# Hymba step: two feed-forward rows started together on four weight tiles, and the next weights loaded in another order

## The chip, the cores and the metric

The kernel runs on one NeuronCore of a Trainium2 chip. A core has engines that work side by side, each in the order of its own instruction list: TensorE (PE, matrix products), VectorE (DVE), ScalarE (ACT), GpSimd (POOL) and SyncE (SP, which here only issues DMAs). The metric is the device time of one execution in microseconds, smaller is better; the time before is the median of three runs.

## The reference

One layer of a decoder, for 512 prompt tokens and 8 sequences of 4 new tokens (544 columns in all), width 1024, feed-forward width 2816, in float32:

```python
def swiglu(x, wg, wu, wd):
    return (jax.nn.silu(x @ wg) * (x @ wu)) @ wd

x = layer_norm(ALPHA * x + 0.5 * swiglu(x, ffn1_wg, ffn1_wu, ffn1_wd), ln1_g, ln1_b)
proj = x @ w_in                   # RWKV-7 heads and a short convolution
...                               # state update, group norm, gates
x = layer_norm(ALPHA * x + mix, ln2_g, ln2_b)
x = layer_norm(ALPHA * x + 0.5 * swiglu(x, ffn2_wg, ffn2_wu, ffn2_wd), ln3_g, ln3_b)
```

The change is in the first `swiglu`, and in the loading that the second shares with it.

## The kernel before, in words

**Three products for one.** Each float32 matrix is split into a high part (`hl[:, 0]`, written by ACT with rounding to the format `F32R`) and a low part (`hl[:, 1]`, the difference, written by DVE). `wsplit` does it for weights (L133, L134), `split` for inputs (L137, L138). A product is then three matmuls: high by high, high by low, low by high (`mm3`, L149 to L151).

**The feed-forward layers.** The class `Ffn` works on the 2816 hidden values in 22 rows of 128. Each row has a tile of gate weights (`"g"`) and one of up weights (`"u"`), 512 KB each. `up(m, h)` computes row m for half h of the columns (half 0 is columns 0 to 255, half 1 is 256 to 543): 24 matmuls with the gate tile, the silu on ACT (L324), 24 with the up tile, the multiplication on DVE (L328). Rows 0 to 3 are chunk 0 and are computed so, directly. Later chunks are computed in pairs of rows with fewer products, from sums and differences of weight blocks: `pairs` and `downs` go through `prod` (L464 to L466), and a table of events, sorted by due time, says when each combined weight is made. A counter `t` counts the products; each piece of weights is loaded (`load`, L407 and L409) as x and a, the block b is split off the x, a GpSimd DMA adds another block to the x in place (L437, L443), a and x are split, DVE adds a into the x (L430, L431), and the y so made is split too. Evacuations of PSUM in these parts are L525, L531, L534, L570 and L573 on ACT.

**Buffers in turns.** Raw weights come into five buffers of 512 KB that are used strictly in turns, in the order in which the program asks for them (`ring`); the split tiles use six others in the same way. A DMA whose buffer is still in use waits on SP, and what stands behind it on SP waits too. `feed(n)` asks for pieces as long as fewer than n are held, then makes those that are due. In layer 1 (`nf` = 2) the first half of rows 0 and 1 comes ahead of `main`; rows 2 and 3 are done in `main`, which asks for the weights of each row when it gets there. After row 2 `main` sets `t` to -5 and calls `feed(2)`, so that the first four pieces (two of down weights for each of two groups) are asked for ahead of row 3's tiles. In layer 2 (`nf` = 4) all rows' weights are asked for ahead of `main`.

**The order of work.** The code is a recording: a scheduler arranges each engine's instructions by its own estimate of times, and on each engine they then run in that order. The instruction orders below are the result of that.

## Time and profile before

| | |
|---|---|
| median of three runs | 1148.94 us |
| the runs | 1146.88, 1148.94, 1152.93 us |
| profiled execution | 1144.4 us, span 1142.3 us, mean granted clock 0.992 |
| PE busy | 1106.8 us (97%) |
| DVE busy | 857.2 us (75%) |
| ACT busy | 586.1 us (51%) |
| first matmul of the first half of row 0 | 4.72 us |
| first matmul of the second half of row 0 | 20.85 us |

Times within the profile count from the start of the span. A row of the timeline gives the start, the length, the engine (SPq is SP's queue), the line of the kernel, the operation with the tiles it writes and reads, and in brackets how long the engine had been idle and what ended that. `hl` and `hlb` are split weights, `raw` are weights as loaded, `xhl` is the split input, `tv` and `hhl` are split inputs of the later chunks, `cpb` and `sv` are scratch. A matmul's length in the row overlaps with the next, so the distance from start to start is what PE needs for one.

### The profile page before, as it was taken

The page shows a single profiled execution, that of the slowest core. Times are in us where ns is not written, and L with a number is a line of the kernel's source. Part 1 is how long each engine was busy: PE and PEld are TensorE (multiplying, and loading weights), DVE is VectorE, ACT ScalarE, POOL GpSimd, SP SyncE. Part 2 cuts the span into 40 slices and gives each one's busy share as a digit, 9 for nine tenths or more (in the row PEclk, how much of TensorE's full clock was granted, in tenths as well). Part 3 has the DMA queues.
Part 4 walks back from the last instruction along what each step waited for, and adds up shares of the span by engine and source line. Part 5 has one row for each costly group of instructions (what it writes and reads, how often), then busy time and mean ns, then how long its engine had stood idle before and what let it go on. Part 6 is the DMA issues. An engine that isn't in the chain of part 4 may idle for free.

```text
span 1142.3 us, 22932 instructions
## 1 busy us (share of the span) xinstructions
PE 1106.8 (97%) x9300; PEld 1049.3 (92%) x9300; DVE 857.2 (75%) x1602; ACT 586.1 (51%) x1066; POOL 174.2 (15%) x282
## 2 busy tenths in 40 slices
PE   8999999999999999999999999899999999999995
PEld 7999999999999999898788878899999999999995
DVE  7677988879776867745577368988979888787755
ACT  6545555564553476553245343657555555545523
POOL 0021131312100032221011100001222212121000
PEclk9999999999999999999999999999999999999998
DMA  8557594957742242262128423353675949577302
GB/s 281 119 112 168 131 219 116 200 149 166 163 145 78 92 132 66 53 121 78 48 66 223 118 76 96 130 184 63 130 180 124 228 97 217 148 161 167 105 1 79
DMA packets 97626, 149.32 MB, mean 131 GB/s; under 512 B 35056, under 2 KB 58992, under 8 KB 97520
## 3 DMA queue, kind: packets, MB, share of 16 engines
q1 hardware_dynamic: 70320, 111.67, 32.3%
q0 software_dynamic: 27200, 36.18, 20.2%
q8 instruction: 73, 1.20, 0.4%
q14 instruction: 33, 0.27, 0.1%
HBM read 129.17 MB, written 9.75 MB: 122 GB/s over the span
## 4 chain that ended last, share of the span: by engine, by line
PE 68%; DMA 10%; DVE 10%; issue 7%; ACT 5%; SPq 0%; ACTq 0%; POOL 0%; POOLq 0%; DVEq 0%
PE mm L149 7%; PE mm L464 7%; PE mm L151 7%; PE mm L465 6%; PE mm L466 6%; PE mm L150 6%; DMA raw<-in_gu 6%; PE sm L464 5%; PE sm L466 5%; PE sm L465 5%; DVE hl L134 2%; ACT hl L133 2%; PE sm L929 1%; DMA z<-in_xT 1%; PE sm L208 1%
## 5 line engine op out<-in xcount | busy, mean ns | idle before, releaser
L134 DVE TENSOR_TENSOR hl<-raw,hl 128x1024 fp32r<-128x1024 f32 (+3 forms) x228 | 269.5, 1189 | 67.0 <-ACT hl L133 64.8
L133 ACT ACTIVATE hl<-raw 128x1024 fp32r<-128x1024 f32 (+3 forms) x228 | 231.5, 1027 | 86.2 <-DVE raw L431 32.5
L149 PE MATMUL mm<-xhl,hl 128*128 128x256 f32 (+1 forms) x768 | 235.6, 307 | 8.4 <-ACT xhl L137 4.9
L151 PE MATMUL mm<-xhl,hl 128*128 128x256 f32 (+1 forms) x768 | 227.8, 298 | 1.4 <-DVE hl L134 1.4
L150 PE MATMUL mm<-xhl,hl 128*128 128x256 f32 (+1 forms) x768 | 226.4, 295 | 0.6 <-DVE xhl L231 0.3
L149 PEld LDWEIGHTS mm<-xhl,hl 128*128 128x128 f32 x768 | 147.4, 192 | 16.6 <-ACT xhl L137 5.2
L150 PEld LDWEIGHTS mm<-xhl,hl 128*128 128x128 f32 x768 | 147.5, 192 | 6.5 <-issue 1.6
L151 PEld LDWEIGHTS mm<-xhl,hl 128*128 128x128 f32 x768 | 147.0, 192 | 5.8 <-DVE hl L134 2.4
L464 PE MATMUL sm<-xhl,hl 128*128 128x272 f32 x432 | 124.7, 289 | 0.0
L466 PE MATMUL sm<-xhl,hl 128*128 128x272 f32 x432 | 124.6, 289 | 0.0
L465 PE MATMUL sm<-xhl,hl 128*128 128x272 f32 x432 | 124.6, 288 | 0.0
L464 PE MATMUL mm<-tv,hl 128*128 128x272 f32 x288 | 83.7, 291 | 3.5 <-ACT cpb L525 2.9
L466 PE MATMUL mm<-tv,hl 128*128 128x272 f32 x288 | 83.6, 290 | 0.0
L465 PE MATMUL mm<-tv,hl 128*128 128x272 f32 x288 | 82.5, 286 | 0.0
L466 PEld LDWEIGHTS sm<-xhl,hl 128*128 128x128 f32 x432 | 81.6, 189 | 0.0
L443 POOL DMA_DIRECT2D raw<-in_wd x32 | 39.3, 1494 | 277.2 <-DVE hlb L138 275.4
L465 PEld LDWEIGHTS sm<-xhl,hl 128*128 128x128 f32 x432 | 81.3, 188 | 0.0
L464 PEld LDWEIGHTS sm<-xhl,hl 128*128 128x128 f32 x432 | 81.3, 188 | 0.0
L437 POOL DMA_DIRECT2D raw<-in_gu x36 | 43.4, 1206 | 238.4 <-DVE hlb L138 131.7
L464 PEld LDWEIGHTS mm<-tv,hl 128*128 128x128 f32 x288 | 54.1, 188 | 5.0 <-ACT cpb L525 3.5
L464 PE MATMUL mm<-hhl,hl 128*128 128x272 f32 x192 | 57.0, 302 | 1.7 <-ACT sv L570 1.6
L464 PE MATMUL sm<-hhl,hl 128*128 128x272 f32 x192 | 55.9, 291 | 0.0
(367 smaller groups left out, 2818.9 us busy)
## 6 DMA issues: line engine op xcount, KB each, us to landing
raw<-in_gu SPq DMA_DIRECT2D x86, 512.0 KB, 5.0
raw<-in_gu POOLq DMA_DIRECT2D x36, 512.0 KB, 7.4
raw<-in_wd SPq DMA_DIRECT2D x32, 512.0 KB, 4.8
raw<-in_win SPq DMA_DIRECT2D x26, 512.0 KB, 3.6
raw<-in_wd POOLq DMA_DIRECT2D x32, 256.0 KB, 6.5
raw<-in_wd SPq DMA_DIRECT2D x16, 384.0 KB, 3.3
z<-cpb POOLq DMA_DIRECT2D x16, 272.0 KB, 8.7
z<-sv POOLq DMA_DIRECT2D x16, 272.0 KB, 5.7
```

The source lines that it names most:

```text
L133: ACT.activation(hl[:, 0, a:b], raw[:, a:b], AF.Copy)
L134: DVE.tensor_tensor(hl[:, 1, a:b], raw[:, a:b], hl[:, 0, a:b].bitcast(F32), op=OP.subtract)
L149: PE.matmul(out, wh, src[:, 0, k, c0:c1], start=(i == 0), stop=False)
L150: PE.matmul(out, wh, src[:, 1, k, c0:c1], start=False, stop=False)
L151: PE.matmul(out, wl, src[:, 0, k, c0:c1], start=False, stop=(i == n - 1))
L208: PE.matmul(v[:, :n], ones, qq[:, i, :], start=(j == 0 and i == 0), stop=(j == 3 and i == 1))
L437: POOL.dma_start(x.rearrange("p (s c) -> p s c", s=2), bass.AP(tensor=a11.tensor, offset=a11.offset, ap=[[2 * D, P], [P * 2 * D, 2], [1, 5 ...
L443: POOL.dma_start(four(x)[:, i], bass.AP(tensor=a11.tensor, offset=a11.offset, ap=[[DFF, P], [P * DFF, 2], [1, 256]]), accum_op=OP.add)
L464: PE.matmul(out, wh, src(0, i), start=(first and i == 0), stop=False, skip_group_check=True)
L465: PE.matmul(out, wh, src(1, i), start=False, stop=False, skip_group_check=True)
L466: PE.matmul(out, wl, src(0, i), start=False, stop=(i == n - 1), skip_group_check=True)
L929: PE.matmul(q[r0:r0 + m, o:o + nn], lhs, rhs, start=True, stop=True)
```

## The change

The first half of rows 0 and 1 is no longer done tile after tile. All four weight tiles come in pieces of two, two and four of the eight input blocks, interleaved with the input, and `first_rows` goes through the input blocks in pairs and takes the four tiles in turns for each pair, with four accumulators in PSUM. Ahead of it come an activation with one element (which loads ACT's silu table), a memset and four full-precision matmuls on zeros whose result is not used. In `main`, layer 1 asks for row 3's tiles after row 1, and both layers ask for up to five pieces ahead instead of two. The same products are computed, with the same sizes.

```diff
+        def first_rows(self, o):
+
+            for a, b in ((0, 2), (2, 4), (4, 6), (6, 8)):
+                for i in range(4):
+                    hl = self.w["gu"[i % 2], i // 2]
+                    for k in range(a, b):
+                        for j, (v, y) in enumerate(((0, 0), (0, 1), (1, 0))):
+                            PE.matmul(o[i][:, :256], block(hl, v, k), xhl[:, y, k, 0:256], start=(k == 0 and j == 0),
+                                      stop=(k == KD - 1 and j == 2), skip_group_check=True)
+            for m in range(2):
+                s = self.rows[0][:, m, 0:256]
+                ACT.activation(s, o[2 * m][:, :256], AF.Silu)
+                DVE.tensor_tensor(s, s, o[2 * m + 1][:, :256], op=OP.mult)
+            yield 0
+
...
                 yield from self.up(m, 1)
                 next(tv)
-                if i == 2 or i == 1 and self.nf == self.na:
+                if i == 1 and self.nf < self.na:
+                    for j, n in enumerate("gu"):
+                        self.w[n, 3] = wload(self.gu[3, :, j, :])
+                elif i in (1, 2):
                     self.t = (-12, -5)[i - 1]
-                    self.feed(2)
+                    self.feed()
...
     f1.open()
-    raw, hl = wtiles()
-    f1.w["g", 0] = hl
+    ACT.activation(warm, one, AF.Silu)
+    POOL.memset(cpb[:, 0:256], 0.0)
+    firsts = [sm() for _ in range(4)]
+    for _ in range(4):
+        PE.matmul(firsts[0][:, :256], cpb[:, 0:P], cpb[:, 0:256], start=True, stop=True)
+    ws = [wtiles() for _ in range(4)]
+
+    def first_w(i, a, b):
+        raw, hl = ws[i]
+        dma(raw[:, a * P:b * P], gu1[i // 2, :, i % 2, a * P:b * P])
+        wsplit(hl, raw, a * P, b * P)
+
+    def first_x(a, b, c0, c1):
+        dma(z[:, a:b, c0:c1], xT[:, a:b, c0:c1])
+        split(xhl[:, 0, a:b, c0:c1], xhl[:, 1, a:b, c0:c1], z[:, a:b, c0:c1])
+
+    for a, b in ((0, 2), (2, 4), (4, 8)):
+        first_w(0, a, b)
+        first_x(a, a + 2, 0, 256)
+        first_w(1, a, b)
+        if b - a > 2:
+            first_x(a + 2, b, 0, 256)
+        first_w(2, a, b)
+        first_w(3, a, b)
+    for i, key in enumerate((("g", 0), ("u", 0), ("g", 1), ("u", 1))):
+        f1.w[key] = ws[i][1]
     for k in range(0, KD, 2):
-        dma(raw[:, k * P:(k + 2) * P], gu1[0, :, 0, k * P:(k + 2) * P])
-        dma(z[:, k:k + 2, 0:256], xT[:, k:k + 2, 0:256])
-        wsplit(hl, raw, k * P, (k + 2) * P)
-        split(xhl[:, 0, k:k + 2, 0:256], xhl[:, 1, k:k + 2, 0:256], z[:, k:k + 2, 0:256])
-    f1.w["u", 0] = wload(gu1[0, :, 1, :], 1024, 2)
-    f1.w["g", 1] = wload(gu1[1, :, 0, :])
-    f1.w["u", 1] = wload(gu1[1, :, 1, :])
-    for k in range(0, KD, 2):
-        dma(z[:, k:k + 2, 256:T], xT[:, k:k + 2, 256:T])
-        split(xhl[:, 0, k:k + 2, 256:T], xhl[:, 1, k:k + 2, 256:T], z[:, k:k + 2, 256:T])
+        first_x(k, k + 2, 256, T)
+    for i, n in enumerate("gu"):
+        f1.w[n, 2] = wload(gu1[2, :, i, :])
     dma(vc, vec)
     dma(ones, cst[:, C_ONES:C_ONES + P])
-    drain(f1.first(), f1.main())
+    drain(f1.first_rows(firsts), f1.main())
```

**SP, the first weights and inputs.** SP's list at its beginning; the number behind a tile's name tells buffers' uses apart, in the order of the program. Before, a quarter of row 0's gate tile (`raw_91`) and a quarter of the input's first half (`z`) alternate, and the other three tiles come whole or in halves:

```order
L633 DMA raw_91<-in_gu1 128x256
L634 DMA z_77<-in_xT 128x2x256
L116 DMA raw_117<-in_gu1 128x512 x2
L116 DMA raw_125<-in_gu1 128x1024
L116 DMA raw_130<-in_gu1 128x1024
L641 DMA z_77<-in_xT 128x2x288 x4
```

Now (`raw_101`, `103`, `105` and `107` are the four tiles), the first and the last group:

```order
L657 DMA raw_101<-in_gu1 128x256
L661 DMA z_77<-in_xT 128x2x256
L657 DMA raw_103<-in_gu1 128x256
L657 DMA raw_105<-in_gu1 128x256
L657 DMA raw_107<-in_gu1 128x256
L657 DMA raw_101<-in_gu1 128x512
L657 DMA raw_103<-in_gu1 128x512
L657 DMA raw_105<-in_gu1 128x512
L657 DMA raw_107<-in_gu1 128x512
L661 DMA z_77<-in_xT 128x2x288 x4
```

Ahead of the input's second half (the last row of each) there were 12 DMAs, eight alternating quarters and four for the other three tiles; now there are 16, with the same bytes.

**SP, row 3's tiles and the pieces.** Before, from row 2's tiles on: `raw_535` and `raw_540` are row 3's, `511` to `533` the four down pieces, `681`, `683` and `685` the first pieces of chunk 1 (x and a of its first pair, x of its second), `769` and `771` the next two:

```order
L409 DMA raw_511<-in_wd1 128x2x512
L409 DMA raw_513<-in_wd1 128x2x512
L409 DMA raw_531<-in_wd1 128x2x512
L409 DMA raw_533<-in_wd1 128x2x512
L116 DMA raw_535<-in_gu1 128x1024
L407 DMA raw_681<-in_gu1 128x1024
L116 DMA raw_540<-in_gu1 128x1024
L407 DMA raw_769<-in_gu1 128x1024
L407 DMA raw_771<-in_gu1 128x1024
L407 DMA raw_683<-in_gu1 128x1024
L407 DMA raw_685<-in_gu1 128x1024
```

Now row 3's are `409` and `414`, the down pieces `539` to `545`, and chunk 1's `547`, `565`, `567`, `787`, `789`:

```order
L116 DMA raw_409<-in_gu1 128x1024
L116 DMA raw_414<-in_gu1 128x1024
L424 DMA raw_539<-in_wd1 128x2x512
L424 DMA raw_541<-in_wd1 128x2x512
L424 DMA raw_543<-in_wd1 128x2x512
L424 DMA raw_545<-in_wd1 128x2x512
L422 DMA raw_547<-in_gu1 128x1024
L422 DMA raw_565<-in_gu1 128x1024
L422 DMA raw_567<-in_gu1 128x1024
L422 DMA raw_787<-in_gu1 128x1024
L422 DMA raw_789<-in_gu1 128x1024
```

Row 3's tiles moved ahead of the down pieces, and chunk 1's pieces now come in the order in which they are used.

**ACT, rows 2 and 3.** `sv` is row 2's and 3's result, `hlb` the b block of a piece. Before, around row 2's silu:

```order
L133 ACTIVATE hl_536<-raw_535 128x1024
L137 ACTIVATE hhl_88<-hk_89 128x272
L137 ACTIVATE tv_256<-cpb_71 128x544
L133 ACTIVATE hl_526<-raw_511 128x1024
L324 ACTIVATE sv_90<-mm_391 128x256
L137 ACTIVATE hlb_712<-raw_681 128x512
```

Now:

```order
L137 ACTIVATE hlb_705<-raw_543 128x512
L137 ACTIVATE hlb_730<-raw_547 128x512
L324 ACTIVATE sv_90<-mm_419 128x256
L133 ACTIVATE hl_557<-raw_539 128x1024
L137 ACTIVATE hhl_88<-hk_89 128x272
L137 ACTIVATE tv_284<-cpb_71 128x544 x2
```

The split of the b block of chunk 1's first piece (`hlb_712`, now `hlb_730`) moved from behind row 2's first silu to ahead of it. From the end of chunk 0 on all engines have the same instructions in the same order as before, but for a few in the first pairs of chunk 1.

## The prediction

> **What bounds the kernel now.** The page comes first.

> ```profile
> span 1142.3 us, 22932 instructions
> PE 1106.8 (97%) x9300; PEld 1049.3 (92%) x9300; DVE 857.2 (75%) x1602; ACT 586.1 (51%) x1066; POOL 174.2 (15%) x282
> ```

> TensorE (PE) is busy 97% of the span, so the kernel ends when PE has issued its last matmul. The change can only take away time in which PE stands or issues slowly. The sum of busy and idle by stretch (columns: stretch, length, busy time and count of PE, PEld, DVE, ACT, POOL, granted clock, DMA share, GB/s) shows the beginning:

> ```profile
> 0.00:4.72 4.72, 0.00 (x1) 0.01 (x1) 0.45 (x2) 2.38 (x4) 0.40 (x8) 1.00 0.52 146
> 4.72:12.03 7.31, 6.84 (x25) 5.65 (x25) 5.04 (x9) 4.92 (x9) 0.00 (x0) 1.00 0.99 310
> 12.03:20.85 8.82, 8.79 (x73) 8.59 (x73) 6.87 (x11) 5.92 (x10) 0.00 (x0) 1.00 1.05 380
> 20.85:48.00 27.15, 27.15 (x215) 27.15 (x214) 20.95 (x38) 17.65 (x30) 5.01 (x4) 1.00 0.68 165
> ```

> Busy time misleads here: 24 matmuls fill 4.72 to 12.03, and 72 of the same size fill the 8.82 us behind it. Next to the pitch of starts, the timeline of PE shows where it stood (start, length, instruction, and in brackets the idle time and what ended it):

> ```profile
> 4.72 0.58 PE L149 MATMUL mm<-xhl,hl 128*128 128x256 f32 x1 [4.72 <-ACT xhl L137]
> 11.60 0.41 PE L150 MATMUL mm<-xhl,hl 128*128 128x256 f32 x1
> 11.82 0.38 PE L151 MATMUL mm<-xhl,hl 128*128 128x256 f32 x1
> 12.03 0.28 PE L149 MATMUL mm<-xhl,hl 128*128 128x256 f32 x1
> 12.15 0.28 PE L150 MATMUL mm<-xhl,hl 128*128 128x256 f32 x1
> 20.85 0.30 PE L149 MATMUL mm<-xhl,hl 128*128 128x288 f32 x1
> 48.31 0.28 PE L151 MATMUL mm<-xhl,hl 128*128 128x256 f32 x1
> 49.13 0.39 PE L149 MATMUL mm<-xhl,hl 128*128 128x256 f32 x1 [0.54 <-ACT hl L133]
> 49.36 0.28 PE L150 MATMUL mm<-xhl,hl 128*128 128x256 f32 x1
> 50.39 0.39 PE L151 MATMUL mm<-xhl,hl 128*128 128x256 f32 x1 [0.76 <-DVE hl L134]
> 76.36 0.29 PE L465 MATMUL mm<-xhl,hl 128*128 128x272 f32 x1
> 78.27 0.39 PE L464 MATMUL mm<-hhl,hl 128*128 128x272 f32 x1 [1.62 <-ACT sv L570]
> 85.52 0.28 PE L466 MATMUL sm<-xhl,hl 128*128 128x272 f32 x1
> 88.40 0.39 PE L464 MATMUL mm<-tv,hl 128*128 128x272 f32 x1 [2.59 <-ACT cpb L525]
> 834.99 0.29 PE L466 MATMUL sm<-xhl,hl 128*128 128x272 f32 x1
> 836.25 0.39 PE L464 MATMUL mm<-tv,hlb 128*128 128x272 f32 x1 [0.98 <-ACT cpb L534]
> ```

> The pitch is 0.22 us at 11.60 and 0.12 us from 12.03 (8.82 / 72 = 0.1225 with one small wait, 0.1185 without). So the first half of rows 0 and 1 takes 20.85 - 4.72 = 16.1 us where 96 x 0.1185 = 11.4 us would do. Behind it come three stands in the first feed-forward layer, each counted as start to start less a pitch, plus 0.1 us for the slow start after it: row 3 loses (0.82 - 0.12) + (1.03 - 0.12) + 0.2 = 1.8 us, the one at 78.27 1.9 us, the one at 88.40 2.85 us. The last two rows are the second layer, to which I come back.

> What the three stands wait for is in the rows of SP, ACT and POOL:

> ```profile
> 42.78 0.33 SPq L116 DMA_DIRECT2D raw<-in_gu  x1
> 48.02 1.06 ACT L133 ACTIVATE hl<-raw 128x1024 fp32r<-128x1024 f32 x1 [0.24 <-DMA raw<-in_gu]
> 77.31 0.63 ACT L137 ACTIVATE hlb<-raw 128x512 fp32r<-128x512 f32 x1 [2.72 <-DMA raw<-in_gu]
> 78.96 1.21 POOL L437 DMA_DIRECT2D raw<-in_gu  x1 [5.00 <-DVE hlb L138]
> 85.11 2.95 ACT L133 ACTIVATE hl<-raw 128x1024 fp32r<-128x1024 f32 x3 [3.62 <-DMA raw<-in_gu]
> ```

> Row 3's second tile is issued only at 42.78, because its buffer (of five, in turns) holds the first down piece until that has been split. Its split at 48.02 is what PE waits for. Since row 3's two tiles stand in the turns behind four pieces, the third piece of the next chunk (the x of pair 1) comes into a buffer that is free only past 70 us: it lands at 77.3, its accumulating DMA leaves at 78.96 and lands at 85.1, and ACT, which works in order, has the evacuations for which PE waits (L570, L525) behind these two.

> **The change, part by part.**

> *The start.* Deliveries and splits are priced by these rows (DMA: count, size, time from issue to landing; two stretches, in which the flow begins; splits: mean ns of one):

> ```profile
> z<-in_xT SPq DMA_DIRECT2D x4, 256.0 KB, 4.5
> raw<-in_gu SPq DMA_DIRECT2D x4, 128.0 KB, 3.5
> 1.00:2.00 1.00, 0.00 (x0) 0.00 (x0) 0.00 (x0) 1.00 (x1) 0.00 (x0) 1.00 0.08 15
> 2.00:3.00 1.00, 0.00 (x0) 0.00 (x0) 0.00 (x0) 0.03 (x1) 0.00 (x0) 1.00 0.77 207
> 9.39 0.63 ACT L137 ACTIVATE xhl<-z 128x512 fp32r<-128x512 f32 x1 [0.27 <-DMA z<-in_xT]
> L133 ACT ACTIVATE hl<-raw 128x512 fp32r<-128x512 f32 x2 | 1.3, 631 | 0.0
> L134 DVE TENSOR_TENSOR hl<-raw,hl 128x512 fp32r<-128x512 f32 x2 | 1.3, 692 | 0.0
> ```

> The same 96 matmuls now stand in four groups of 24, and what they need together is four tiles of 512 KB and 1 MB of input, 3072 KB in 16 DMAs where the first tile and the input had 8. Before, the first 1536 KB had landed by 9.39. The other 1536 KB at the 380 GB/s of the 12.03 row take 4.0 us more: the last quarter pair lands at 13.4. Then 0.63 (ACT), 0.69 (DVE), four matmuls on that half (0.5) and the whole last group (24 x 0.1185 = 2.85): PE ends the first half at 18.1, and with small waits on the second half of the input at 18.35. That half has its own chain: DVE has to make four lower parts, with a plan input and two multiplications between; I get its last at 20.5, and PE needs it 18 matmuls into the next row, at 20.7. So it is just covered; a DVE that is 1 us later costs 0.8. Saved: 20.85 - 18.35 = **2.5 us**. The ends: at best PE runs fast from 5.4 on (5.4 + 11.4 = 16.8, **4.1 us**), at worst PE is slow until 12.03 as before: 31 matmuls at 0.21 from 5.44, then 65 x 0.1185, end 19.75, **1.1 us**. I lean to the middle since by the deliveries the clock hardly matters: a slow first group ends at 10.5, before the third group's tiles are there.

> *The warm-up.* It has to be free:

> ```profile
> L208 PE MATMUL sm<-lnq,ones 128*128 128x256 f32 x16 | 3.7, 386 | 1.4 <-ACT lnq L204 1.4
> L883 POOL MEMSET De<- 128x256 f32 x2 | 0.6, 310 | 39.8 <-DVE z L223 39.8
> ```

> The 16 rows are 8 full-precision matmuls, 0.46 us each at the fast pitch. Four of them at half speed take 3.7 us; behind a 0.31 us memset that can begin at 0.9 they run from 1.3 to 5.0, in the 4.72 us in which PE has nothing. Without that cover they cost 0.3 us. The early activation loads a table that ACT otherwise loads at 11.35; PE did not wait for that one, so I count nothing. What the row of 12.03 says of the clock is that PE was slow for 7.3 us of work with small gaps. [...]

> *Row 3 early.* Both tiles are issued right behind row 2's and split at about 27 and 30.5 us; row 3 begins at about 43. The 1.8 us go: **1.8 us**. If only the first tile came in time, 0.9.

> *Pieces in clean turns.* The two stands of 1.9 and 2.85 us go, and the question is what is late next. The second layer has just this order (all its weights ahead of all pieces), so it serves as price. From the first evacuation of its first chunk to that of the second:

> ```profile
> 64.98 0.40 ACT L570 ACTIVATE cpb<-mm 128x272 f32<-128x272 f32 x1 [1.57 <-PE mm L466]
> 133.94 0.40 ACT L570 ACTIVATE cpb<-mm 128x272 f32<-128x272 f32 x1 [1.59 <-PE mm L466]
> 808.49 0.40 ACT L570 ACTIVATE cpb<-mm 128x272 f32<-128x272 f32 x1 [1.11 <-PE mm L466]
> 874.28 0.40 ACT L570 ACTIVATE cpb<-mm 128x272 f32<-128x272 f32 x1 [1.60 <-PE mm L466]
> ```

> Layer 1 takes 68.96 us, layer 2 65.79: **3.2 us** between them. Layer 2 still has the stand at 836.25 (1.25 us), which layer 1 now hides behind its own. I expect it to come up at the same place, so the term is 3.2 and not 4.75. Ends: 4.75 if no stand comes up, 2.3 if two do.

> *The second layer* loads five pieces ahead instead of two. The instructions of every engine stand there in the same order as before, and SP reaches the DMAs no earlier than their buffers are free: nothing, and no more than its 1.25 us either way.

> **The sum:** 2.5 + 1.8 + 3.2 = 7.5 us. From the profiled execution, 1144.4 us (span 1142.3), that is 1136.9. This execution lies 4.5 us under the median 1148.94 of the three runs (1146.88 to 1152.93); from the median the forecast is **1141.4 us**. With the ends: 1.1 + 1.8 + 2.3 = 5.2 to 4.1 + 1.8 + 4.75 = 10.65, or 1143.7 to 1138.3.

> **The rivals.**

> *All stands go* and the start is at its best: 10.65 us, 1138.3. For it: the later chunks of layer 1 run without a stand. Against it: layer 2's stand in the same order.

> *PE stays slow to 12 us.* 1.1 + 1.8 + 3.2 = 6.1, 1142.8. For it: before, 7.3 us of work did not suffice. Against it: PE now works without a gap from 1.3.

> *The start is starved.* 16 smaller DMAs run at the rate of the first 1536 KB (from about 2.2, in the second of the two stretches, to 9.39: 213 GB/s) all the way: the last lands at 2.2 + 3072 / 213 = 16.6, PE ends at 21.3, 0.45 us after 20.85. Sum 4.55, 1144.4. For it: those rows, and four more DMAs ahead of the second input half. Against it: 380 GB/s as soon as rows of 2 KB and more come. [...]

> *Slower:* a piece ahead of its time stops ACT. The x of pair 0 is now split (hlb) ahead of row 2's first silu, and PE needs that silu for the third matmul group after it, at about 39.9. Its DMA leaves when DVE has split row 3's second tile, about 30.7, and by this row lands at 37:

> ```profile
> raw<-in_gu SPq DMA_DIRECT2D x5, 512.0 KB, 6.3
> ```

> So 2 us are spare, and from there each us costs PE one. It eats the gain from 9.5 us of lateness on; at 12 us (its buffer free only after layer 1's first y split, as row 3's tile had it) the time is 2.5 us above the median, 1151.4. For it: DVE is nearly full from 14 to 31 us. Against it: that buffer's last user in the new order is row 3's tile, not a piece.

> **How the numbers follow.** Likeliest 0.50; all go 0.15; slow clock 0.20; starved 0.10; slower 0.05. About 0.5% (5.7 us, below 1143.2) is what a measurement of this kernel tells from no change. The runs before spread over 6 us, so a median of three moves by some 2 us: faster then has 0.78 in the likeliest case, 0.95 when all goes, 0.55 with the slow clock, 0.4 when starved, in sum 0.68; I write 0.66, same 0.30, slower 0.04. The range takes the ends (1138.3 and 1144.4) and that 2 us on each side: 1136.5 to 1147.0.

> **What would show it.** Right: the first 128x288 matmul at about 18.3 us; no wait of row 3 on hl; from there to the first L570 of the next chunk no waits but one of about 1 us at the evacuation that is L534 now; the rest shifted as a whole by 7 to 8 us. Wrong: the first 128x288 matmul past 20; a wait of PE near 40 us behind a split of a piece; or a stand beyond 100 us that was not there. If the stands go and the end does not move, the later stages are not bound by PE as the 97% suggest.

## The result and the profile after

The changed kernel takes 1140.53 us in the median (1134.12 to 1150.78, 20 executions), the kernel before 1147.89 us (1143.24 to 1154.22, 20 executions on the same chip). The ratio is 0.9934 with a 95% interval of 0.9914 to 0.9955; of 1147.9 us the change saves 7.6, between 5.2 and 9.9. The forecast was 1141.4 us.

The page of the changed kernel begins so. Its profiled execution took 1138.5 us, 5.9 us less than the one before, and its span is 5.5 us shorter:

```profile
span 1136.8 us, 22970 instructions
PE 1107.5 (97%) x9308; PEld 1049.5 (92%) x9308; DVE 857.2 (75%) x1606; ACT 585.4 (51%) x1070; POOL 175.1 (15%) x283
```

The timeline of PE shows the start, the one stand that is left ahead of the second chunk's end, and the same place in the second layer:

```profile
1.25 3.78 PE L652 MATMUL sm<-cpb 128*128 128x256 f32 x8 [1.25 <-POOL cpb L649]
4.90 7.57 PE L360 MATMUL sm<-xhl,hl 128*128 128x256 f32 x49
12.80 5.83 PE L360 MATMUL sm<-xhl,hl 128*128 128x256 f32 x47 [0.34 <-DVE xhl L138]
18.47 0.30 PE L149 MATMUL mm<-xhl,hl 128*128 128x288 f32 x1
87.18 0.29 PE L481 MATMUL sm<-xhl,hl 128*128 128x272 f32 x1
90.28 0.39 PE L479 MATMUL mm<-tv,hlb 128*128 128x272 f32 x1 [2.81 <-ACT cpb L549]
828.63 0.29 PE L481 MATMUL sm<-xhl,hl 128*128 128x272 f32 x1
830.00 0.39 PE L479 MATMUL mm<-tv,hlb 128*128 128x272 f32 x1 [1.08 <-ACT cpb L549]
```

The first 128x288 matmul starts at 18.47 us (20.85 before). Row 3 no longer waits, and neither does PE at the two places in the second chunk where it stood for 1.9 and 2.9 us. But at the evacuation that is L549 now it stands for 3.10 us from start to start, where 1.25 us were forecast. SP and ACT show why (the SP row is the wait and issue of six DMAs in a row):

```profile
44.24 34.80 SPq L422 DMA_DIRECT2D raw<-in_gu  x6
86.83 0.63 ACT L137 ACTIVATE hlb<-raw 128x512 fp32r<-128x512 f32 x1 [4.95 <-DMA raw<-in_gu]
88.89 1.06 ACT L133 ACTIVATE hl<-raw 128x1024 fp32r<-128x1024 f32 x1 [1.42 <-DVE raw L446]
89.85 0.38 ACT L549 ACTIVATE cpb<-mm 128x272 f32<-128x272 f32 x1
```

The last of the six DMAs is issued at 79.04 (44.24 + 34.80) and lands at 86.83. ACT works in order and has the b split of this piece, the chunk's fourth, ahead of L549. Behind that split comes one that waits for DVE, and only then the evacuation for which PE waits.

What stands behind the stand is the surprise. The sum by stretch, for 3.9 us behind the stand in the changed kernel and then for 3.6 us behind the 2.9 us stand of the kernel before:

```profile
90.28:94.17 3.89, 3.89 (x18) 3.89 (x19) 3.89 (x5) 2.96 (x5) 0.00 (x0) 0.56 0.95 212
```

```profile
88.40:92.00 3.60, 3.60 (x28) 3.60 (x29) 3.56 (x6) 0.40 (x1) 1.21 (x1) 1.00 1.03 227
```

The granted clock is 0.56, and 18 matmuls start in the time of 31 at the full pitch of 0.126 us. Before, it stayed at 1.00. The stand costs 3.0 us, and the clock behind it 1.5 us more.

From here on one number serves as measure: the start of the first evacuation of the second chunk's end, which is the row of ACT that the prediction quoted at 133.94 us for before. With the change it is

```profile
129.84 0.40 ACT L585 ACTIVATE cpb<-mm 128x272 f32<-128x272 f32 x1 [1.59 <-PE mm L481]
```

so 4.1 us of the gain are made by then, in these two executions. Behind it no code differs that acts (the limit of five pieces in place of two gives the same instruction lists on all engines, row for row).

### The profile page after: what moved, and what is told of

It reads as the page before. It is cut to its first block, busy times and chain, and to the rows that moved or that the text cites. A ratio compares the mean times of both kernels' runs of the same rounds, so it can differ in the third digit from the quotient of the medians.

```text
span 1136.8 us, 22970 instructions
## 1 busy us (share of the span) xinstructions
PE 1107.5 (97%) x9308; PEld 1049.5 (92%) x9308; DVE 857.2 (75%) x1606; ACT 585.4 (51%) x1070; POOL 175.1 (15%) x283
## 4 chain that ended last, share of the span: by engine, by line
PE 72%; DVE 10%; DMA 8%; ACT 5%; issue 4%; SPq 0%; ACTq 0%; POOL 0%; POOLq 0%; DVEq 0%
PE mm L149 7%; PE mm L151 7%; PE mm L150 7%; PE mm L479 7%; PE mm L480 7%; PE mm L481 7%; DMA raw<-in_gu 6%; PE sm L479 5%; PE sm L480 5%; PE sm L481 5%; DVE hl L134 2%; ACT hl L133 2%; PE sm L964 1%; PE sm L208 1%; PE sm L149 1%
## 5 line engine op out<-in xcount | busy, mean ns | idle before, releaser
L134 DVE TENSOR_TENSOR hl<-raw,hl 128x1024 fp32r<-128x1024 f32 (+3 forms) x232 | 269.7, 1171 | 63.8 <-ACT hl L133 63.0
L133 ACT ACTIVATE hl<-raw 128x1024 fp32r<-128x1024 f32 (+3 forms) x232 | 232.0, 1012 | 81.6 <-DVE raw L446 33.3
L149 PE MATMUL mm<-xhl,hl 128*128 128x288 f32 (+1 forms) x736 | 224.2, 305 | 2.9 <-DVE z L1318 1.9
L151 PE MATMUL mm<-xhl,hl 128*128 128x288 f32 (+1 forms) x736 | 216.5, 295 | 0.6 <-DVE hl L134 0.6
L150 PE MATMUL mm<-xhl,hl 128*128 128x288 f32 (+1 forms) x736 | 214.8, 292 | 0.3 <-DVE xhl L231 0.3
L149 PEld LDWEIGHTS mm<-xhl,hl 128*128 128x128 f32 x736 | 139.1, 189 | 10.4 <-DVE z L1318 2.6
L150 PEld LDWEIGHTS mm<-xhl,hl 128*128 128x128 f32 x736 | 139.5, 190 | 5.2 <-issue 1.6
L151 PEld LDWEIGHTS mm<-xhl,hl 128*128 128x128 f32 x736 | 138.8, 189 | 4.6 <-issue 1.6
L479 PE MATMUL mm<-hhl,hl 128*128 128x272 f32 x192 | 57.0, 302 | 0.2
L480 PE MATMUL mm<-hhl,hl 128*128 128x272 f32 x192 | 55.7, 290 | 0.0
## 6 DMA issues: line engine op xcount, KB each, us to landing
raw<-in_gu SPq DMA_DIRECT2D x84, 512.0 KB, 5.0
raw<-in_gu POOLq DMA_DIRECT2D x36, 512.0 KB, 7.9
raw<-in_wd SPq DMA_DIRECT2D x32, 512.0 KB, 4.5
raw<-in_win SPq DMA_DIRECT2D x26, 512.0 KB, 3.6
raw<-in_wd POOLq DMA_DIRECT2D x32, 256.0 KB, 6.3
```

The source lines that it names most:

```text
L133: ACT.activation(hl[:, 0, a:b], raw[:, a:b], AF.Copy)
L134: DVE.tensor_tensor(hl[:, 1, a:b], raw[:, a:b], hl[:, 0, a:b].bitcast(F32), op=OP.subtract)
L149: PE.matmul(out, wh, src[:, 0, k, c0:c1], start=(i == 0), stop=False)
L150: PE.matmul(out, wh, src[:, 1, k, c0:c1], start=False, stop=False)
L151: PE.matmul(out, wl, src[:, 0, k, c0:c1], start=False, stop=(i == n - 1))
L479: PE.matmul(out, wh, src(0, i), start=(first and i == 0), stop=False, skip_group_check=True)
```

## The experiments

**Each half alone.** The first kernel has the new start and the old loading, the second the old start and the new loading:

```diff
 # start_only: the changed kernel with
-                if i == 1 and self.nf < self.na:
-                    for j, n in enumerate("gu"):
-                        self.w[n, 3] = wload(self.gu[3, :, j, :])
-                elif i in (1, 2):
+                if i == 2 or i == 1 and self.nf == self.na:
...
 # plan_only: the kernel before with the same lines the other way round
```

> The changed start alone; row 3's weights and the pieces as in the kernel before. Theory A (the gain is a sum of three separate parts, 2.4 us of it from the start): first 128x288 matmul at 18.5 us, and the stands of row 3 (1.8 us), of L570 (1.9) and of L525 (2.9) are all still there; the span is 2.4 us under that of before. Theory B (the parts depend on each other: rows that begin earlier reach row 3 earlier, while its second tile's buffer comes free at the same time): row 3's stand grows by what the start gained, to about 4 us, and the start alone gains under 0.7 us.

> The start as before; row 3's tiles ahead of the pieces, five pieces ahead. Theory A: first 128x288 matmul at 20.85 us as before, row 3 without a stand, then only the stand of 3.1 us at L534 (the line of the kernel before for L549); gain 1.8 + 4.75 - 3.1 = 3.5 us. Theory B (the stand at L549 is so long because everything now comes 2.4 us sooner): with the old start that stand is only about 1 us, as in layer 2, and this kernel alone gains 5 to 5.5 us, nearly all of the change.

The start alone: 1145.57 us, ratio 0.999 (0.9961 to 1.002). The loading alone: 1139.65 us, ratio 0.9913 (0.988 to 0.9947). By these times nearly all of the gain comes from the loading and next to none from the start. But the 2.4 us that the start was to save lie within the interval of the start alone, so the times do not decide between its theories. The trace speaks against theory B: row 3's stand, which was to grow to about 4 us, takes 1.92 us (1.61 before). The start itself does what it should, the first 128x288 matmul is at 18.66 us. PE of the kernel with the start alone then stands five times:

```profile
47.24 0.38 PE L149 MATMUL mm<-xhl,hl 128*128 128x256 f32 x1 [0.84 <-ACT hl L133]
48.50 0.38 PE L151 MATMUL mm<-xhl,hl 128*128 128x256 f32 x1 [0.76 <-DVE hl L134]
76.57 0.40 PE L479 MATMUL mm<-hhl,hl 128*128 128x272 f32 x1 [1.83 <-ACT sv L585]
86.69 0.40 PE L479 MATMUL mm<-tv,hl 128*128 128x272 f32 x1 [1.05 <-ACT cpb L540]
95.34 0.39 PE L479 MATMUL mm<-tv,hlb 128*128 128x272 f32 x1 [0.84 <-ACT cpb L549]
76.57:81.00 4.43, 4.43 (x23) 4.43 (x24) 3.17 (x6) 2.44 (x5) 1.21 (x1) 0.61 0.44 54
```

The stands are other ones than before but of the same sum, 6.15 us against 6.16 (each start to start, less a pitch of 0.12). What takes 1.6 us of the start's 2.2 back in this execution is the last row: behind the stand of 1.83 us the clock is halved. The kernel with the loading alone has one stand, of 1.39 us where its two theories had 3.1 and about 1, and no halved clock behind it:

```profile
91.40 0.39 PE L464 MATMUL mm<-tv,hlb 128*128 128x272 f32 x1 [1.22 <-ACT cpb L534]
91.40:94.81 3.41, 3.41 (x27) 3.41 (x28) 3.41 (x5) 2.84 (x5) 0.00 (x0) 1.00 0.88 216
87.96 0.63 ACT L137 ACTIVATE hlb<-raw 128x512 fp32r<-128x512 f32 x1 [3.37 <-DMA raw<-in_gu]
```

The clock also hides the start in the times. The record has the span and the mean granted clock of each of these executions. Their product is the span less the time that a halved clock cost, if PE was busy meanwhile, so it is an estimate of the time at full clock. In the mean it is 1133.9 us for the 15 executions of the kernel before, 1131.8 with the start alone and 1131.3 with the loading alone: 2.2 and 2.7 us less (standard errors 0.7 and 0.6). For the loading alone that is less than the 4.5 us that its trace has by the second chunk's end (129.42). Its five executions had lost less to the clock, 6.1 us in the mean against 12.0 before. By this the start is worth about what it was forecast to be.

**Without the warm-up.** The four matmuls on zeros are left out:

```diff
-    for _ in range(4):
-        PE.matmul(firsts[0][:, :256], cpb[:, 0:P], cpb[:, 0:256], start=True, stop=True)
```

> The change without the four matmuls on zeros. Theory A (the start is bound by deliveries: 256 KB each 0.69 us from 10.7 on): PE is at the slow pitch until 8 to 12 us, the first group ends at about 10 instead of 8.2, but the first 128x288 matmul is at 18.5 to 19.0, as good as unchanged. Theory B (the clock sets the start's end): slow until 12 us as in the kernel before, end at 19.7 or later, 1.2 us lost.

Measured: 1139.89 us, ratio 0.9912 (0.9881 to 0.9943), not to be told from the change. Two stretches of the start, without the warm-up and then with it, show what it does:

```profile
6.00:8.00 2.00, 2.00 (x12) 2.00 (x10) 1.16 (x3) 0.88 (x3) 0.00 (x0) 1.00 0.99 342
8.00:10.00 2.00, 2.00 (x12) 2.00 (x12) 1.46 (x4) 1.42 (x4) 0.00 (x0) 1.00 0.99 283
10.00:12.00 2.00, 2.00 (x20) 2.00 (x19) 1.29 (x3) 1.29 (x3) 0.00 (x0) 1.00 0.99 322
```

```profile
6.00:8.00 2.00, 2.00 (x20) 2.00 (x19) 1.00 (x3) 0.86 (x3) 0.00 (x0) 1.00 1.03 326
8.00:10.00 2.00, 1.88 (x13) 1.36 (x12) 1.45 (x4) 1.44 (x4) 0.00 (x0) 1.00 0.87 265
```

With it PE is at 20 matmuls in 2 us from 6 us on, but then starves at 8 to 10 us. Without it PE is slow until about 10 us and has work all the time. The first 128x288 matmul comes at 18.95 in place of 18.47: the warm-up is worth 0.5 us, since the deliveries bound the start.

**The stand at L549.** What ACT waits for there is a split that PE needs only later. This kernel has it three products later, in the table of lead times:

```diff
-LEAD_B = {0: 25, 1: 23}
+LEAD_B = {0: 25, 1: 23, 3: 15}
```

> The change with the b block of the fourth row pair member (u = 3) made 15 instead of 18 products ahead, in every chunk of both layers; on ACT the split then stands behind the evacuation L549 instead of ahead of it. Theory A (the stand of 3.1 us in layer 1 and of 1.4 us in layer 2 is ACT waiting in order for a piece that PE does not need yet): both stands go or fall under 0.3 us and the span is 4 us under that of the change. Theory B (the piece itself is late): PE stands later instead, at the product with that b block or with the y made after it, and the span stays within 1 us.

Measured: 1138.55 us, ratio 0.9893 (0.9828 to 0.9958). ACT now evacuates first, and the stand is gone in both layers:

```profile
84.94 0.38 ACT L549 ACTIVATE cpb<-mm 128x272 f32<-128x272 f32 x1
87.42 0.63 ACT L137 ACTIVATE hlb<-raw 128x512 fp32r<-128x512 f32 x1 [0.66 <-DMA raw<-in_gu]
125.58 0.40 ACT L585 ACTIVATE cpb<-mm 128x272 f32<-128x272 f32 x1 [1.59 <-PE mm L481]
```

The piece still lands at 87.4. The span of this execution, 1142.1 us, does not show the gain, since the clock is halved from 518.8 to 546.1 us, in code that is the same. So the stand came from the order on ACT together with a late piece, and the order alone removes it. The second chunk's end comes 4.3 us earlier than with the change, 8.4 us earlier than before.

**Why the piece is late.** Two additions into z run on the DMA engines just then. This kernel cuts them from 272 to 16 columns, in this group alone, and so leaves out part of layer 1's sum:

```diff
-                    POOL.dma_start(z[:, ds[q]:ds[q] + 2, TB:], cp[q], accum_op=OP.add)
+                    w = 16 if self.ph == "1" and (ci, g) == (0, 1) else TB
+                    POOL.dma_start(z[:, ds[q]:ds[q] + 2, TB:TB + w], cp[q][:, :, 0:w], accum_op=OP.add)
```

> The changed kernel, with two additions of layer 1 thinned: the two DMAs of L596 that add the second group of chunk 0 into z at about 80.5 us carry 16 columns in place of 272, so that part of layer 1's sum is left out. Order and waits stay as they are. Theory D (the DMA engines are shared): the x whose split stops ACT at 86.83 lands late because its 512 KB compete with those 544 KB; without them it lands 1.5 to 2 us earlier, at about 85, the stand at L549 shrinks from 2.8 to 1.3 us or less and the clock stays full behind it; first L585 of the second chunk at about 126.8. Theory E (the issue sets it): it lands at 86.8 and the stand stays 2.8 us; first L585 at 129.8.

Measured: 1143.34 us, ratio 0.995 (0.9912 to 0.9987). Theory D fell. The rows of ACT and PE:

```profile
86.23 0.63 ACT L137 ACTIVATE hlb<-raw 128x512 fp32r<-128x512 f32 x1 [4.26 <-DMA raw<-in_gu]
89.68 0.39 PE L479 MATMUL mm<-tv,hlb 128*128 128x272 f32 x1 [2.12 <-ACT cpb L549]
89.68:93.00 3.32, 3.32 (x26) 3.32 (x27) 3.32 (x5) 2.85 (x5) 0.00 (x0) 1.00 0.90 219
```

The piece, issued at 79.49, lands at 86.23. The changed kernel itself, profiled once more beside it, had it issued at 79.50, landed at 86.37 and a stand of 2.10 us of idle time. So those bytes are not the cause; the two additions still ran, so this does not say that they cost nothing. Over five traces the stand follows the time from issue to landing: 7.8 us and 3.10 us from start to start, 7.9 and 3.14 without the warm-up, 6.9 and 2.39, 6.7 and 2.41 here, 5.8 and 1.51 with the old start. What sets that time between 5.8 and 7.9 us is still open.

**The changed kernel and the later split, with more executions, and the later split with the old start:**

> The changed kernel itself, for comparison on the same chip. Theory C: 4.1 us from the traces and 2.6 us for the clock that the profiled execution before escaped, 6.7 us in all, ratio 0.994; its stand of 2.8 us halves the clock for 3.41 us in nearly every execution. Theory T: 4.1 us, ratio 0.9964. In its trace the stand at L549 of 2.8 us again, and behind it 14 or 15 matmuls at a pitch of 0.23 us.

> The changed kernel with the b split of each chunk's fourth piece asked for three products later (lead 15 in place of 18), once more and with more executions. In the traces so far the first L570 or L585 of layer 1's second chunk starts at 133.94 us before, 129.84 with the change, 125.58 with this. Theory C (the clock): a stand of PE also halves the clock for 3.41 us, worth 1.71 us, when about 1.45 us of it fall into one 3.41 us window of a raster that runs by itself. The two stands of 1.62 and 2.59 us in the kernel before would then do this in about 62% and 91% of its executions, (3.41 - 1.62 + 0.34)/3.41 and (3.41 - 2.59 + 2.28)/3.41, though the profiled one escaped both: 2.6 us that its trace does not show. Gain over before: 8.4 + 2.6 + 1.35 for layer 2's stand = 12.3 us, ratio 0.989. Theory T (the traces alone): 8.4 + 1.35 = 9.7 us, ratio 0.9915. No stand at the evacuation that is L549 in either layer, under both.

> The kernel before with the change in the loading of rows 2 and 3 and the later b split, and with the old start. Theory A: the start's 2.4 us count in full as soon as PE waits for no delivery behind it: the first 128x288 matmul at about 21.2 us (18.82 with the new start), the first L570 of the second chunk at 127.9 (125.58), the whole 2.4 us longer than with the new start. Theory B: the deliveries of the second chunk set the pace whatever PE does, and the start is lost there in any case: first L570 of the second chunk at 125.6 to 126.1, the same time as with the new start.

Measured in this order: 1144.73 us, ratio 0.9958 (0.9922 to 0.9994); 1135.73 us, 0.9874 (0.9835 to 0.9913); 1134.42 us, 0.9859 (0.9824 to 0.9894). By the traces the start counts in full once no stand is left: the second chunk's end is at 125.65 us with the new start and at 127.69 with the old one. The times do not show these 2.0 us, so the pair was taken again:

> The changed kernel with the later b split a third time, beside the one with the old start: does the start show in the times where no stand is behind it? Theory A: 2.0 us by the traces (first L585 of the second chunk at 125.6 against 127.7), so 2 us faster than the one with the old start. Theory B: no difference or the other sign, as in the first pair (1135.73 against 1134.42).

> The old start with the new loading and the later b split, again. First 128x288 matmul at 20.9 to 21.2, first L570 of the second chunk 106.8 us behind it, no stand between. Theory A: 2 us slower than with the new start. Theory B: the same or faster.

This time the new start gave 1128.88 us, ratio 0.9832 (0.979 to 0.9873), the old one 1134.42 us, 0.9876 (0.9831 to 0.9921). The traces repeat to 0.1 us (125.58 and 127.67). The first pair has the new start 1.3 us slower, the second 5.5 us faster: executions of one kernel spread over 5 to 17 us, and 2 us do not show in pairs of six. With the clock taken out as above they do: span times granted clock is 1122.6 us in the mean with the new start and 1124.7 with the old one in the first pair, 1121.5 and 1123.8 in the second. That is 2.1 and 2.3 us (standard errors 0.9 and 0.7), as the traces have it.

**Is it the idle time that halves the clock?** This kernel gives PE 16 matmuls to do during the stand, ahead of the product that waits for L549. Their result is not used:

```diff
+                if self.ph == "1" and ci == 1 and u == 0:
+                    fill = sm()[:, :TB]
+                    for _ in range(16):
+                        PE.matmul(fill, xhl[:, 0, 0, 0:P], xhl[:, 0, 0, 0:TB], start=True, stop=True, skip_group_check=True)
                 yield from prod(b1, u, "b", 0, tb(2), False)
```

> The changed kernel with 16 matmuls more, whose result is not used, ahead of the product that waits for the evacuation L549 in layer 1's second chunk. They take 16 x 0.126 = 2.0 us and stand where PE waits 2.1 to 2.85 us anyway; all other lists are the same. In eight of the traces so far the start of the second chunk's end (the first L570 or L585 of the chunk) is the start of the first 128x288 matmul, plus the stands, plus 106.8 to 106.9 us where the clock stayed full, or 108.35 to 108.55 where it was halved behind a stand. Theory C (it is PE's idleness within one 3.41 us window that halves the clock): the wait ends when it did, but is under 0.9 us of idle, so the pitch behind it is 0.126 from the start, and that rest is 106.8 to 107.0. Theory F (the slow matmuls behind the stand come from something else that the stand goes with: DMA traffic, operands, the evacuation): the pitch is 0.23 for some 14 matmuls again, rest 108.4.

Measured: 1138.48 us, ratio 0.9916 (0.9881 to 0.995). The rows of PE and the stretch behind them:

```profile
87.31 0.29 PE L481 MATMUL sm<-xhl,hl 128*128 128x272 f32 x1
87.44 2.16 PE L515 MATMUL sm<-xhl 128*128 128x272 f32 x16
90.17 0.39 PE L479 MATMUL mm<-tv,hlb 128*128 128x272 f32 x1 [0.57 <-ACT cpb L553]
90.17:93.58 3.41, 3.41 (x27) 3.41 (x28) 3.41 (x5) 2.85 (x5) 0.00 (x0) 1.00 0.99 216
```

It came out as theory C said. The product waits as long as without the 16 (2.86 us from 87.31 to 90.17), at the same traffic, and the clock stays at 1.00 behind it. The second chunk's end is at 128.19. But this one execution does not show that the 16 did it. Counted in windows of 3.4133 us from the halved one at 457.27 (the last section says why), a window begins at 88.63 here, so the empty stand would have been cut into 1.0 and 1.5 us, and windows with so much idle time were followed by a halved clock only about half of the time (17 of 34 with 1.39 to 1.77 us).

Against theory F speak two traces in which the same stand has the same length. In the second trace of the change its 2.10 us fall into one window (87.33 to 90.75), and the next is halved:

```profile
89.82 0.39 PE L479 MATMUL mm<-tv,hlb 128*128 128x272 f32 x1 [2.10 <-ACT cpb L549]
89.82:93.40 3.58, 3.58 (x19) 3.58 (x20) 3.58 (x5) 2.84 (x5) 0.00 (x0) 0.63 0.91 219
```

In the kernel with the thinned additions a window begins at 89.20 and cuts the 2.12 us into 1.64 and 0.48, and at the same 219 GB/s the clock stays at 1.00, in the rows above.

All traces together fit one sum: the second chunk's end is the first 128x288 matmul, plus the stands, plus 106.8 us of work, plus 1.5 us where the clock was halved once (us; stands from start to start, less 0.12 to 0.13 each, the filled one too; bold where the clock was halved):

| kernel | first 128x288 | stands | second chunk's end | rest |
|---|---|---|---|---|
| before | 20.85 | 6.16 | 133.94 | 106.93 |
| the change | 18.47 | 2.98 | 129.84 | **108.39** |
| the change, again | 18.72 | 2.27 | 129.34 | **108.35** |
| start alone | 18.66 | 6.15 | 133.35 | **108.54** |
| loading alone | 21.17 | 1.39 | 129.42 | 106.86 |
| no warm-up | 18.95 | 3.02 | 130.37 | **108.40** |
| additions into z thinned | 18.53 | 2.29 | 127.70 | 106.88 |
| stand filled | 18.58 | 2.74 | 128.19 | 106.87 |
| later split (three) | 18.82 to 18.90 | 0 | 125.58 to 125.65 | 106.75 to 106.76 |
| later split, old start (two) | 20.91 to 20.92 | 0 | 127.67 to 127.69 | 106.76 to 106.77 |

## Why the prediction was right, and where it was wrong

The time was right: 1141.4 us were forecast, 1140.5 measured. But that it came so close is in part luck: one of the three terms came to next to nothing in the traces, and part of the measured gain comes from something that was not in the sum.

- **The start, 2.5 us:** measured 2.38 (18.47 against 18.35 forecast). The third group's pieces come one per 256 KB, 0.69 to 0.73 us apart, and ACT splits each as it lands:

```profile
10.70 0.63 ACT L133 ACTIVATE hl<-raw 128x512 fp32r<-128x512 f32 x1 [1.26 <-DMA raw<-in_gu]
11.39 0.64 ACT L137 ACTIVATE xhl<-z 128x512 fp32r<-128x512 f32 x1
12.08 0.63 ACT L133 ACTIVATE hl<-raw 128x512 fp32r<-128x512 f32 x1
12.79 0.64 ACT L137 ACTIVATE xhl<-z 128x512 fp32r<-128x512 f32 x1
13.47 1.36 ACT L133 ACTIVATE hl<-raw 128x512 fp32r<-128x512 f32 x2
```

  The last row holds two splits; the second starts at 14.20, when the last piece has landed, 0.8 us later than the 13.4 of the prediction. It cost nothing, because PE did not wait for it: PE's last wait ends at 12.80, for the low part of the input piece that is split at 11.39, and behind it the 47 matmuls of that row of PE's timeline run without a gap. So the end fits to 0.1 us although the path through the last piece does not. Without the warm-up PE comes to 20 matmuls in 2 us at 10 us in place of 6, and the end is only 0.5 us later, so deliveries rather than the clock bound the start, as forecast. The rivals of a slow PE (end at 19.75) and of a starved start (21.3) are out. With work from 1.25 on PE is fast from about 6 us (20 matmuls in 6.00:8.00); before, with work from 4.72 on, its pitch came to 0.12 us only at 12.03.
- **Row 3, 1.8 us:** its two stands are gone, 1.61 us by start to start. Right.
- **Pieces in clean turns, 3.2 us:** this is the step that failed. The two stands went as forecast (1.79 and 2.76), and the stand that was to come up did come up, at the very evacuation that was named. But it was priced at 1.25 us by the second layer and took 2.98, and the halved clock behind it 1.46 more (108.39 less 106.93). The term was 1.79 + 2.76 - 2.98 - 1.46 = 0.1 us. The price from the second layer was wrong in two ways: the fourth piece takes 7.8 us from issue to landing here and 6.3 us there (issued 820.27, landed 826.55), and the price of a stand held 0.1 us for the slow start behind it where a halved clock takes 1.5.
- **The second layer, nothing:** right. From its first chunk's end to its second's it takes 65.89 us, 65.79 before.
- **The sum:** 2.38 + 1.61 + 0.1 = 4.1 us, just what the second chunk's end shows, and not 7.5 or the shift of 7 to 8 us that the prediction named as its sign. The profiled spans differ by 5.5, since the kernel before had three stretches of halved clock between there and the second layer, the change one:

```profile
462.55:465.96 3.41, 3.41 (x31) 2.79 (x29) 1.84 (x6) 1.43 (x4) 0.77 (x5) 0.50 0.74 193
629.81:633.22 3.41, 3.41 (x18) 3.41 (x17) 0.00 (x0) 0.43 (x2) 0.00 (x0) 0.50 1.27 236
742.45:745.86 3.41, 3.41 (x17) 3.41 (x16) 2.12 (x5) 0.32 (x1) 0.00 (x0) 0.50 0.77 252
```

```profile
735.84:739.25 3.41, 3.41 (x17) 3.41 (x16) 2.06 (x5) 0.31 (x1) 0.00 (x0) 0.51 0.76 253
```

  That code is the same in both, and so is, for one, the stand ahead of the second of these places (2.31 us of idle time before, 2.35 with the change, which paid nothing there); it is chance, as the last section shows. With the ones at 90.7 and 1121.5 us the change too has three ahead of the last 10 us of its span, so that the clock cancels in the spans: 5.5 us is what start and stands are worth without it, 2.38 + 1.61 + 1.79 + 2.76 - 2.98 = 5.56.
- **Where the rest of 7.6 us comes from** is not shown. It may be noise: 5.5 us lie within the measured 5.2 to 9.9, and the change's second measurement gave 4.8 us (0.7 to 9.0). One argument is that the 4.1 us hold for one execution each, and the one before was lucky. Its stands of 1.6 and 2.6 us both escaped the halved clock, which stands of that size do not always do. If a window with 1.45 us of idle time halves the clock, they do so in 62% and 91% of the executions, as the expectation of the later split's second measurement works out; with 1.65 us it is 0% and (3.41 - 2.59 + 1.88)/3.41 = 79%. At 1.55 us each that is an estimate of 1.2 to 2.4 us on average. With it the change is worth 5.3 to 6.5 us. No run here counted how often those two stands pay, and the clocks on record do not bear it out: in the second measurement the kernel before lost 11.4 us to the clock in the mean, the change 15.7, and span times granted clock still differs by 7.6 us (standard error 0.5). Some 2 us of that are left without an explanation.
- **The rivals:** *all stands go* is what the later split made of it, at 1128.9 to 1138.6 us in three measurements against the forecast of 1138.3. *Slower, by the early piece ahead of row 2's silu:* PE has no wait near 40 us, so that piece was in time.

The kernel with the later split beats both: its ratios to the kernel before are 0.9893, 0.9874 and 0.9832, and where it ran beside the change (0.9874 and 0.9958) the intervals do not overlap.

## What to carry to other kernels

When a change removes stands from an engine that works in order, look for the load-bound instruction that stands ahead of the next evacuation, and move it behind. Price what comes up by its own delivery, not by a place with the same order elsewhere. Price a stand of TensorE with the clock behind it (here a halved window took 1.5 us more, behind 17 of 34 windows with 1.39 to 1.77 us of idle time and 14 of 15 with 1.82 us or more), and where it can't be removed, useless matmuls in it may keep the clock, which the one execution here does not show. Before two kernels are told apart by 2 us, compare the granted clocks of their executions.

## What the runs showed of the hardware

```profile
91.67:95.08 3.41, 3.41 (x18) 3.41 (x17) 3.11 (x5) 2.01 (x5) 0.00 (x0) 0.51 1.06 236
624.15:627.56 3.41, 3.41 (x20) 3.41 (x17) 0.00 (x0) 0.43 (x2) 0.00 (x0) 0.51 1.28 216
736.79:740.20 3.41, 3.41 (x17) 3.41 (x16) 2.07 (x5) 0.46 (x1) 0.00 (x0) 0.51 0.78 232
832.43:835.84 3.41, 3.41 (x18) 3.41 (x17) 3.06 (x5) 1.96 (x5) 0.00 (x0) 0.50 1.08 249
```

The ends lie 532.48, 645.12 and 740.76 us behind the first: 156, 189 and 217 times 3.4133 us, to within 0.1 us. The clock records of the trace of before give the three halved stretches ahead of its last 10 us as 3.413 us each, begun at 462.580, 629.833 and 742.473 us: 49 and 33 times 3.4133 us apart. Between them lies all the rest of the kernel, so the raster does not follow the program. I laid it over all 13 traces and took the idle time of PE that falls into each window. Of 57 windows with 0.8 to 1.38 us of it, 1 was followed by a halved clock; of 34 with 1.39 to 1.77 us, 17; of 15 with 1.82 us or more, 14. So it is not the length of a stand that decides but how the raster cuts it: the 2.59 us stand of the kernel before is cut into 1.31 and 1.28 us and costs nothing more, the 2.81 us of the change fall into one window.

**It also makes executions differ.** Where the raster lies at the start of an execution is chance: in the three traces of the later split its first window behind the start of the span begins at 3.38, 0.73 and 2.29 us (counted back from the first release of the clock at 6.79, 4.14 and 5.70; in the traces of before and of the change that release, at 12.02 and 5.33 us, lies 132 and 25 windows ahead of the first halved one, at 462.58 and 90.66). So each of a kernel's stands pays some 1.5 us or nothing. The record bears this out: 23 executions of the kernel before on one chip have spans of 1142.6 to 1155.2 us, and span times granted clock goes only from 1133.3 to 1139.3 us. In the state updates, at 515 to 545 and 640 to 670 us, where matmuls are short, several traces have the clock halved for two to eight windows in a row with little idle time ahead (two from 517.6 us in the third trace of the later split, behind a stand of 1.13 us; eight from 518.8 in its first; in its second, slow matmuls from 642.4 on, behind 8 us of timeline in which PE does not wait); what decides there was not tried.
